# Expert rows loaded, cast and split 1024 columns at a time, a finish of gathered tokens in seven steps, and a power on one column

## Chip, core and metric

The kernel runs on one core of one Trainium2 chip. The metric is the time on the device in microseconds (us). Engines are named as the profile does: PE is TensorE (PEld its weight loads), DVE is VectorE, ACT is ScalarE, POOL is GpSimd, SP is SyncE, which issues most DMAs.

## The reference

One decoder layer over 512 tokens of width 2048: two mixers, then an expert feed-forward (PEER), then a final RMS norm. What matters here is the expert part. Each token picks 8 x 16 of 16384 experts; `u_emb` and `v_emb` are tables of 16384 rows of 2048 floats.

```python
q = (xb @ w_query).reshape(PEER_BLOCK, PEER_HEADS, 2, PEER_HALF)
...
top_s, pos = lax.top_k(cand_s, PEER_TOPK)
eidx = jnp.take_along_axis(cand_i, pos, axis=-1)
gates = jax.nn.softmax(top_s, axis=-1)
u = u_emb[eidx]
act = jax.nn.gelu(jnp.einsum('ld,lhkd->lhk', xb, u), approximate=False)
return jnp.einsum('lhk,lhkd->ld', gates * act, v_emb[eidx])
```

## The kernel before

Up to about 1320 us the mixers run; then the queries and top-k of the expert part (to about 1610 us); the change begins there. The 512 tokens are treated in two ways.

**Dense tokens.** For the first 320 tokens (`TD`) every expert is computed. `expert_u(i)` multiplies 128 rows of u with the tokens: 16 column blocks, each of three 320-column products (`mm3`, lines 203 to 205: high x high, high x low, low x high), so 48 products into one `mm` tile, then a gelu (line 1152). `expert_v(grp)` does 4 such blocks of v: four quarters q of 512 output columns, 48 products each into four `po` tiles, which VectorE adds to `hT` (line 1222). So one expert_u is a **unit** of 48 products, and one quarter of expert_v another. The weights go through `load_split` or its twin in `expert_v`: a DMA of 128 x 512 floats into `wr`/`vr` (10 buffers, `NRAW`), a ScalarE cast to `whi`/`vhi` (line 199), a GpSimd subtraction to `wlo`/`vlo` (line 200), 4 buffers of each (`NSPL`). Such a piece is 12 products.

**Gates.** Before expert_v can begin, `gate_block` builds for every dense token a 128 x 128 table of gates as a product of two one-hot matrices `J` and `I2` (J for four tokens in one VectorE instruction, line 1130; I2 by VectorE for odd tokens, line 1136, and by two ScalarE instructions for even ones, lines 1139 and 1140; product `pg`, line 1141), which goes through DRAM (`glD`) and comes back by group as `gd`. Meanwhile the first 36 expert_u run (`NSP`), their results waiting in DRAM (`actD`). `expert_g` multiplies them with the gates and splits the product into `ghi` and `glo` (8 buffers of each).

**Gathered tokens.** For the last 192 tokens (`TG`) only the chosen rows are fetched: `gather` issues an indirect DMA of 1 MB on GpSimd's queue into one of six `g` buffers (`NGB`). A u token costs VectorE two multiplications of 128 x 1024 (line 1254); a v token costs TensorE four small products `pw` (line 1268). `pace` is called once per unit, 256 times in all (36 in the gate stage, 32 in the first eight groups, which hold only expert_v, then 188), and issues gathers so that the 384 are used up at unit `NGU`. When 64 tokens are done, `end_steps` adds them to the residual and normalises them, in 5 steps of a unit each; its `norm` raises 128 x 64 numbers to -0.5 on GpSimd (line 1309).

Each engine works its queue in order. A scheduler with its own estimate of times sets that order when the program is built, from pool sizes and dependences.

## Time and profile before

| what | us |
|---|---|
| median of 3 runs (lowest, highest) | 4036.59 (4035.16, 4037.14) |
| the profiled execution | 4028.36 |
| its span in the trace | 4026.3 |
| PE busy | 3661.0 (91%) |
| POOL busy | 2547.7 (63%) |
| DVE busy | 2398.0 (60%) |
| ACT busy | 1521.6 (38%) |

Busy time is a mean over stages of different kinds, so it only says that TensorE is the engine to follow. Products overlap in TensorE's pipeline: one lasts longer than the distance to the next, and a stretch that is busy throughout is not yet one in which every product follows at the shortest distance.

### The profile page before, as it was taken

Reading aid. Unit: us, or ns where it says so; the run is one execution under the profiler, and the core shown is the slowest. Engines: PE = TensorE matmul, PEld = TensorE weight load, DVE = VectorE, ACT = ScalarE, POOL = GpSimd, SP = SyncE. Lnnn points to the kernel's source line nnn. Section 1 sums busy time; section 2 is a strip of 40 time slices with the busy share of each in tenths; the row PEclk is TensorE's granted clock in tenths of the full one; section 3 lists DMA queues with packets and bytes.
Section 4 is the critical chain, followed back from the end, with each engine's and each line's share of the span. In section 5 each row is a group of like instructions: output and inputs, shape, how many; then the busy total and the mean of one; then the engine's idle time right before and its main releaser. Section 6 shows DMA issues by size and latency. Waiting matters only on the chain. (4 is left out here: it accounts for less than half of the span.)

```text
span 4026.3 us, 65357 instructions
## 1 busy us (share of the span) xinstructions
PE 3661.0 (91%) x23705; PEld 3044.2 (76%) x23705; DVE 2398.0 (60%) x4504; ACT 1521.6 (38%) x3090; POOL 2547.7 (63%) x1921
## 2 busy tenths in 40 slices
PE   5899999999999896888978999989999998999998
PEld 3667756766657896887867788877888887888898
DVE  7543154666633799988666676665666656642324
ACT  3444323443333411666533333333333333334433
POOL 5445443333315533666767798878888888887676
PEclk8999999998979998999989999989999999999999
DMA  8465653333253322988998999988998998899743
GB/s 335 169 205 189 209 165 75 85 92 116 77 192 93 122 72 66 334 297 296 345 329 313 329 341 347 341 294 322 329 338 318 338 326 312 322 329 305 244 153 121
DMA packets 392370, 964.60 MB, mean 240 GB/s; under 512 B 76080, under 2 KB 141360, under 8 KB 335920
## 3 DMA queue, kind: packets, MB, share of 16 engines
q1 hardware_dynamic: 336752, 557.76, 42.1%
q0 software_dynamic: 55296, 402.68, 26.6%
q8 instruction: 187, 3.06, 0.3%
q14 instruction: 135, 1.11, 0.1%
HBM read 914.34 MB, written 45.94 MB: 239 GB/s over the span
## 5 line engine op out<-in xcount | busy, mean ns | idle before, releaser
L200 POOL TENSOR_TENSOR wlo<-wr,whi 128x512 fp32r<-128x512 f32 (+2 forms) x832 | 1112.9, 1354 | 842.4 <-ACT whi L199 742.0
L200 POOL TENSOR_TENSOR vlo<-vr,vhi 128x512 fp32r<-128x512 f32 x512 | 710.3, 1408 | 204.7 <-ACT vhi L199 177.9
L205 PE MATMUL mm<-n2hi,wlo 128*128 128x320 f32 x2304 | 742.4, 322 | 96.7 <-POOL wlo L200 96.7
L199 ACT CAST whi<-wr 128x512 fp32r<-128x512 f32 (+2 forms) x832 | 501.3, 616 | 682.1 <-PE mm L204 278.0
L203 PE MATMUL mm<-n2hi,whi 128*128 128x320 f32 x2304 | 741.8, 322 | 12.2 <-ACT whi L199 9.7
L1254 DVE SCALAR_TENSOR_TENSOR g<-g,row 128x1024 f32<-128x1024 f32 x384 | 714.8, 1900 | 33.7 <-DMA g<-in_u,eix 33.7
L204 PE MATMUL mm<-n2lo,whi 128*128 128x320 f32 x2304 | 730.4, 317 | 2.4 <-POOL n2lo L200 2.4
L203 PE MATMUL po<-ghi,vhi 128*128 128x320 f32 x2048 | 626.4, 316 | 35.6 <-DVE hT L1222 23.4
L204 PE MATMUL po<-glo,vhi 128*128 128x320 f32 x2048 | 619.6, 311 | 0.0
L205 PEld LDWEIGHTS mm<-n2hi,wlo 128*128 128x128 f32 x2304 | 447.6, 194 | 152.7 <-POOL wlo L200 138.4
L205 PE MATMUL po<-ghi,vlo 128*128 128x320 f32 x2048 | 475.4, 317 | 23.0 <-POOL vlo L200 22.5
L203 PEld LDWEIGHTS mm<-n2hi,whi 128*128 128x128 f32 x2304 | 449.3, 195 | 43.2 <-issue 24.3
L199 ACT CAST vhi<-vr 128x512 fp32r<-128x512 f32 x512 | 308.2, 619 | 431.9 <-PE mm L204 284.1
L204 PEld LDWEIGHTS mm<-n2lo,whi 128*128 128x128 f32 x2304 | 449.3, 195 | 7.6 <-issue 4.2
L203 PEld LDWEIGHTS po<-ghi,vhi 128*128 128x128 f32 x2048 | 388.1, 190 | 84.4 <-DVE hT L1222 35.0
L1222 DVE SCALAR_TENSOR_TENSOR hT<-po,mod,hT 128x320 f32<-128x320 f32 x512 | 248.3, 544 | 304.8 <-PE po L205 226.6
L1179 DVE TENSOR_TENSOR act<-gd,act 128x320 f32<-128x320 f32 x128 | 150.6, 1183 | 449.1 <-ACT act L1152 435.3
L205 PEld LDWEIGHTS po<-ghi,vlo 128*128 128x128 f32 x2048 | 342.0, 190 | 80.3 <-POOL vlo L200 59.5
L204 PEld LDWEIGHTS po<-glo,vhi 128*128 128x128 f32 x2048 | 388.8, 190 | 3.7 <-issue 3.4
L1247 POOL DMA_INDIRECT g<-in_u,eix x192 | 235.1, 1225 | 103.1 <-DMA eix<-exD 30.8
L203 PE MATMUL mm<-nhi,whi 128*128 128x512 f32 x640 | 261.1, 408 | 4.5 <-ACT whi L199 4.5
L205 PE MATMUL mm<-nhi,wlo 128*128 128x512 f32 x640 | 261.3, 408 | 0.0
(437 smaller groups left out, 5762.1 us busy)
## 6 DMA issues: line engine op xcount, KB each, us to landing
wr<-in_uT SPq DMA_DIRECT2D x512, 256.0 KB
vr<-in_v SPq DMA_DIRECT2D x512, 256.0 KB
wr<-in_wrest SPq DMA_DIRECT2D x160, 256.0 KB
aw<-in_ada SPq DMA_DIRECT2D x32, 1024.0 KB
a2w<-in_adar SPq DMA_DIRECT2D x64, 512.0 KB
glD<-gb SPq DMA_DIRECT2D x10, 2048.0 KB
gd<-glD SPq DMA_DIRECT2D x32, 640.0 KB
a3w<-in_adar SPq DMA_DIRECT2D x32, 512.0 KB
```

Source lines behind the costliest of these rows:

```text
L199: copied.append(S.copy(hi, src))
L200: return (eng or V).tensor_tensor(lo, src, hi.bitcast(F32), OP.subtract)
L203: TE.matmul(ps, lhsT=whi, rhs=xhi, start=first, stop=False)
L204: TE.matmul(ps, lhsT=whi, rhs=xlo, start=False, stop=False)
L205: done_mm[0] = TE.matmul(ps, lhsT=wlo, rhs=xhi, start=False, stop=last)
L1179: V.tensor_tensor(a.rearrange("p (b t) -> p b t", t=TB), gd[:, :, i, :], a.rearrange("p (b t) -> p b t", t=TB), OP.mult)
L1222: V.scalar_tensor_tensor(h, po[d], mod2[:, 48 + k:49 + k], h, OP.mult, OP.add)
L1247: G.indirect_dma_start(out=g, out_offset=None, in_=I[s[0]], in_offset=bass.IndirectOffsetOnAxis(ap=ix, axis=0))
L1254: V.scalar_tensor_tensor(g[:, c], g[:, c], 1.0, n2s[i][:, c], OP.mult, OP.mult, accum_out=wtp[:, e, n:n + 1])
```

## The change

- Rows of u, v and the query weights come in pieces of 1024 columns: one DMA of 512 KB, one cast, one subtraction, 24 products. There are 5 raw buffers and 3 split ones of the double size. v comes from a second copy in DRAM, `vq`, in which such a piece is contiguous.
- `expert_v` has 8 steps of 256 output columns with two `po` tiles each instead of 4 with four; `pace` is called after every second one, so units are as before. The pool of `po` keeps 5 tiles.
- `NGU` is 240 instead of 222. `end_steps` has 7 steps; the power works on 64 x 1 numbers and a transposition spreads the result.
- Smaller stores: `act` 5 instead of 6, `ghi` and `glo` 7 instead of 8, `gd` 1 instead of 2; I2 is one tile per token, 4 of them, instead of 2 tiles for four tokens; `ys` has one buffer in the gate stage; one `cand` instead of 2; the index tables keep only dense tokens.

```diff
 TD = 320
-NGU = 222
+NGU = 240
 TG = T - TD
...
 LEAD = 2
-NRAW = 10
-NSPL = 4
-NACT = 6
+NRAW = 5
+NSPL = 3
+NACT = 5
 NSP = 36
...
     out["v"] = l["peer_v"]
+    out["vq"] = l["peer_v"].reshape(32, 4, P, 8, 2, P).transpose(0, 3, 2, 4, 1, 5)
     return {k: np.ascontiguousarray(v) for k, v in out.items()}
...
-        def project_to(pss, ws, xhi, xlo, ahead=()):
+        def project_to(pss, ws, xhi, xlo, ahead=(), step=4):
...
             ahead = list(ahead)
-            for q in range(0, nk, 4):
-                n = min(4, nk - q)
+            for q in range(0, nk, step):
+                n = min(step, nk - q)
                 for j, ps in enumerate(pss):
...
                         mm3(ps, whi[:, i, :], wlo[:, i, :], xhi[k], xlo[k], k == 0, k == nk - 1)
-                if parts:
-                    parts.pop(0)()
+                        if parts and i % 4 == 3:
+                            parts.pop(0)()
             return last
...
         def query(pss, n0):
-            for q in range(0, KT, 4):
+            for q in range(0, KT, 8):
                 for j, ps in enumerate(pss):
-                    whi, wlo, _ = load_split(I["wq"][n0 + j], q, 4)
-                    for i in range(4):
+                    whi, wlo, _ = load_split(I["wq"][n0 + j], q, 8)
+                    for i in range(8):
                         k = q + i
...
                             jT[:, t0:t0 + 4].unsqueeze(2).to_broadcast([P, 4, P]), OP.is_equal)
-            I2 = gx.tile([P, 4, P], F32, name="I2", bufs=2)
             for i in range(4):
+                I2 = gx.tile([P, P], F32, name="I2", bufs=4)
                 t = t0 + i
                 if i % 2:
-                    V.tensor_scalar(I2[:, i], iota, iT[:, t:t + 1], gT[:, t:t + 1], OP.is_equal, OP.mult)
+                    V.tensor_scalar(I2, iota, iT[:, t:t + 1], gT[:, t:t + 1], OP.is_equal, OP.mult)
                 else:
-                    S.activation(I2[:, i], iota, AF.Abs, bias=iT[:, t:t + 1], scale=-1.0)
-                    S.activation(I2[:, i], I2[:, i], AF.Relu, bias=gT[:, t:t + 1], scale=ngT[:, t:t + 1])
-                TE.matmul(ps[:, i], lhsT=J[:, i], rhs=I2[:, i], start=True, stop=True)
+                    S.activation(I2, iota, AF.Abs, bias=iT[:, t:t + 1], scale=-1.0)
+                    S.activation(I2, I2, AF.Relu, bias=gT[:, t:t + 1], scale=ngT[:, t:t + 1])
+                TE.matmul(ps[:, i], lhsT=J[:, i], rhs=I2, start=True, stop=True)
             S.copy(gb[:, :, 4 * q:4 * q + 4], ps.rearrange("p t i -> p i t"))
...
         ps = pu.tile([P, T], F32, name="mm", tag="mm")
-        last = project_to([ps[:, 0:TD]], I["uT"][i:i + 1], nhi, nlo)
+        last = project_to([ps[:, 0:TD]], I["uT"][i:i + 1], nhi, nlo, step=8)
         acts[i] = va.tile([P, TD], F32, name="act")
...
     late = []
-    ended = [0]
     def expert_g(grp):
-        gd = vp.tile([P, TD // TB, 4, TB], F32, name="gd", bufs=2)
+        gd = vp.tile([P, TD // TB, 4, TB], F32, name="gd", bufs=1)
         nc.sync.dma_start(gd, glD.rearrange("b j i t -> j b i t")[:, :, 4 * grp:4 * grp + 4, :])
...
                             a.rearrange("p (b t) -> p b t", t=TB), OP.mult)
-            ghi = vp.tile([P, TD], F32R, name="ghi", bufs=8)
-            glo = vp.tile([P, TD], F32R, name="glo", bufs=8)
+            ghi = vp.tile([P, TD], F32R, name="ghi", bufs=7)
+            glo = vp.tile([P, TD], F32R, name="glo", bufs=7)
             split(ghi, glo, a, V)
...
-    vrows = I["v"].rearrange("(g i j) c -> g j i c", i=4, j=P)
     def expert_v(grp):
...
         gh = ghl.pop(grp)
-        for q in range(4):
-            po = [pv.tile([P, TD], F32, name="po") for _ in range(4)]
+        for q in range(8):
+            vr = wp.tile([P, 2, 4, P], F32, name="vr", tag="wr", bufs=NRAW)
+            nc.sync.dma_start(vr, I["vq"][grp, q])
+            vhi = wp.tile([P, 2, 4, P], F32R, name="vhi", tag="whi")
+            vlo = wp.tile([P, 2, 4, P], F32R, name="vlo", tag="wlo")
+            last = split(vhi, vlo, vr, G)
+            po = [pv.tile([P, TD], F32, name="po") for _ in range(2)]
             for i in range(4):
-                vr = wp.tile([P, 512], F32, name="vr", tag="wr", bufs=NRAW)
-                nc.sync.dma_start(vr, vrows[grp][:, i, 512 * q:512 * q + 512])
-                vhi = wp.tile([P, 512], F32R, name="vhi", tag="whi")
-                vlo = wp.tile([P, 512], F32R, name="vlo", tag="wlo")
-                last = split(vhi, vlo, vr, G)
-                for d in range(4):
-                    cs = slice(P * d, P * d + P)
-                    mm3(po[d], vhi[:, cs], vlo[:, cs], *gh[i], i == 0, i == 3)
-                if parts:
+                for d in range(2):
+                    mm3(po[d], vhi[:, d, i, :], vlo[:, d, i, :], *gh[i], i == 0, i == 3)
+                if parts and i % 2:
                     parts.pop(0)()
-            if grp == 31:
-                sqs = vp.tile([P, 4, TD], F32, name="gd", bufs=2)
-            for d in range(4):
-                k = 4 * q + d
+            if grp == 31 and q % 2 == 0:
+                sqs = vp.tile([P, 4, TD], F32, name="gd", bufs=1)
+            for d in range(2):
+                k = 2 * q + d
                 h = hT[k]
...
                 if grp == 31:
-                    t = sqs[:, d, :] if k else sacc[:, 0:TD]
+                    t = sqs[:, k % 4, :] if k else sacc[:, 0:TD]
                     S.activation(t, h, AF.Square)
...
                         V.tensor_tensor(sacc[:, 0:TD], sacc[:, 0:TD], t, OP.add)
+            if q % 2 == 0:
+                continue
             pace(last)
...
                           start=True, stop=True, tile_position=(0, 32 * q))
-            ys = gq.tile([P, T], F32, name="ys", bufs=2)
+            ys = yp[-1].tile([P, T], F32, name="ys", bufs=len(yp))
             S.copy(ys, ps)
...
         held[0] += 2
+        acc = gq.tile([P, TF], F32, name="acc")
+        rn = gq.tile([TF, 1], F32, name="rnf")
...
+        def total():
+            V.tensor_reduce(acc, sq.rearrange("p k t -> p t k"), mybir.AxisListType.X, OP.add)
         def norm():
-            acc = gq.tile([P, TF], F32, name="acc")
-            V.tensor_reduce(acc, sq.rearrange("p k t -> p t k"), mybir.AxisListType.X, OP.add)
             ps = pu.tile([P, T], F32, name="mm", tag="mm")
-            TE.matmul(ps[:, 0:TF], lhsT=ones, rhs=acc, start=True, stop=True)
-            rn = gq.tile([P, TF], F32, name="rnf")
-            V.tensor_scalar(rn, ps[:, 0:TF], 1.0 / D, 1e-6, OP.mult, OP.add)
-            G.tensor_tensor(rn, rn, negh[:, 0:1].to_broadcast([P, TF]), OP.pow)
+            TE.matmul(ps[0:TF, 0:1], lhsT=acc, rhs=ones[:, 0:1], start=True, stop=True)
+            V.tensor_scalar(rn, ps[0:TF, 0:1], 1.0 / D, 1e-6, OP.mult, OP.add)
+            G.tensor_tensor(rn, rn, negh[0:TF, 0:1], OP.pow)
+        def leave():
+            ps = pu.tile([P, T], F32, name="mm", tag="mm")
+            TE.transpose(ps[:, 0:TF], rn.to_broadcast([TF, P]), ident[0:TF, 0:TF])
             for e in range(2):
                 ks = slice(8 * e, 8 * e + 8)
-                V.tensor_tensor(hg[:, ks], hg[:, ks], rn.unsqueeze(1).to_broadcast([P, 8, TF]), OP.mult)
+                V.tensor_tensor(hg[:, ks], hg[:, ks], ps[:, 0:TF].unsqueeze(1).to_broadcast([P, 8, TF]), OP.mult)
             nc.sync.dma_start(out.rearrange("k p t -> p k t")[:, :, TD + TF * f:TD + TF * f + TF], hg)
             held[0] -= 2
-            ended[0] += 1
-        return [load, lambda: None, lambda: add(0), lambda: add(1), norm]
+        return [load, lambda: None, lambda: add(0), lambda: add(1), total, norm, leave]
...
     vp = st.enter_context(tc.tile_pool(name="vp", bufs=2, side="right", reuse_waits="tile"))
+    yp.append(vp)
     for grp in range(32):
```

What this does to GpSimd's queue is seen around the first power in the middle of the last stage. `wlo` and `vlo` are subtractions, `DMA g` are gathers, `rnf` is the power. Before:

```order
L1247 DMA g<-in_u,eix 128x2048
L1247 DMA g<-in_v,eT 128x2048
L200 TENSOR_TENSOR wlo<-wr,whi 128x512 x2
L200 TENSOR_TENSOR vlo<-vr,vhi 128x512
L1247 DMA g<-in_u,eix 128x2048
L200 TENSOR_TENSOR vlo<-vr,vhi 128x512 x3
L1247 DMA g<-in_v,eT 128x2048
L1309 TENSOR_TENSOR rnf<-rnf,negh 128x64
L200 TENSOR_TENSOR wlo<-wr,whi 128x512 x4
L1247 DMA g<-in_u,eix 128x2048
L1247 DMA g<-in_v,eT 128x2048
L1247 DMA g<-in_u,eix 128x2048
```

After, at the same place:

```order
L1252 DMA g<-in_v,eT 128x2048
L1252 DMA g<-in_u,eix 128x2048
L1252 DMA g<-in_v,eT 128x2048
L202 TENSOR_TENSOR wlo<-wr,whi 128x1024
L1252 DMA g<-in_u,eix 128x2048
L202 TENSOR_TENSOR vlo<-vr,vhi 128x1024 x2
L1252 DMA g<-in_v,eT 128x2048
L1316 TENSOR_TENSOR rnf<-rnf,negh 64x1
L202 TENSOR_TENSOR wlo<-wr,whi 128x1024 x2
L1252 DMA g<-in_u,eix 128x2048
L1252 DMA g<-in_v,eT 128x2048
L202 TENSOR_TENSOR vlo<-vr,vhi 128x1024
```

Two subtractions of 1024 columns stand where four of 512 stood, with as many gathers between them, and the power has shrunk from 128x64 to 64x1.

The second place is the end of the gate stage on ScalarE, where `I` are the one-hot matrices of even tokens, `gb` the gate tables leaving PSUM, `act` the gelu that ends an expert_u, `ys` rows of a gathered token. Before, from the last of the one-hot instructions on:

```order
L1139 ACTIVATE I_16076<-iota,iT 128x128 x2
L1142 COPY gb<-pg 128x128x4
L1140 ACTIVATE I_16076<-I_16076,gT,ngT 128x128 x2
L199 CAST whi<-wr 128x512 x3
L1271 COPY ys<-pw 128x512
L199 CAST whi<-wr 128x512
L1142 COPY gb<-pg 128x128x4
L1152 ACTIVATE act<-mm 128x320
L199 CAST whi<-wr 128x512 x2
L1271 COPY ys<-pw 128x512
L199 CAST whi<-wr 128x512 x2
L1152 ACTIVATE act<-mm 128x320
```

After, from the last gelu of the gate stage on:

```order
L1158 ACTIVATE act<-mm 128x320
L1145 ACTIVATE I_15911<-iota,iT 128x128
L1145 ACTIVATE I_15922<-iota,iT 128x128
L1146 ACTIVATE I_15911<-I_15911,gT,ngT 128x128
L1146 ACTIVATE I_15922<-I_15922,gT,ngT 128x128
L201 CAST vhi<-vr 128x1024
L1145 ACTIVATE I_15929<-iota,iT 128x128
L1146 ACTIVATE I_15929<-I_15929,gT,ngT 128x128
L1145 ACTIVATE I_15940<-iota,iT 128x128
L1146 ACTIVATE I_15940<-I_15940,gT,ngT 128x128
L1145 ACTIVATE I_15947<-iota,iT 128x128
L1146 ACTIVATE I_15947<-I_15947,gT,ngT 128x128
```

Before, six of the 36 gelus (two of them shown) follow the last one-hot matrix. After, none does: the last gelu is followed by 25 of the 160 pairs of one-hot instructions (5 shown). TensorE's queue has moved likewise: before, 168 expert_u products stand behind the last gate product; after, the last 54 gate products have no expert_u product among or behind them.

## Rows read from the trace of the kernel before

**Rows 1.** Engine busy time in six stretches, one per stage: us, busy us and count by engine, clock, DMA.

```profile
1613.00:1978.00 365.00, 318.85 (x2149) 300.42 (x2148) 314.41 (x420) 230.34 (x551) 246.90 (x175) 0.96 0.87 317
1978.00:2029.00 51.00, 34.22 (x214) 27.27 (x212) 15.41 (x24) 14.31 (x28) 33.88 (x26) 0.85 0.98 349
2029.00:2339.00 310.00, 279.80 (x1748) 241.62 (x1748) 211.72 (x301) 101.29 (x189) 237.34 (x179) 0.95 0.91 323
2339.00:3582.00 1243.00, 1143.92 (x7467) 998.19 (x7460) 798.19 (x903) 431.27 (x801) 1043.71 (x779) 0.97 0.91 327
3582.00:3793.00 211.00, 211.00 (x1436) 173.87 (x1436) 46.01 (x72) 87.12 (x156) 154.64 (x129) 1.00 0.89 303
3793.00:4010.00 217.00, 209.25 (x1415) 207.17 (x1413) 74.88 (x114) 88.08 (x160) 157.38 (x114) 0.98 0.43 137
```

**Rows 2.** The same view of single groups of the last stage.

```profile
3862.00:3918.00 56.00, 56.00 (x384) 56.00 (x384) 14.89 (x24) 22.56 (x40) 41.20 (x32) 1.00 0.49 161
2610.00:2770.00 160.00, 138.35 (x890) 122.36 (x890) 103.00 (x115) 51.74 (x96) 126.76 (x94) 0.94 0.86 308
3278.00:3366.00 88.00, 74.64 (x480) 65.75 (x479) 61.43 (x63) 28.41 (x53) 70.62 (x49) 0.92 0.80 271
```

**Rows 3.** The same view, only what writes or reads `pw`: PE, PEld, ACT.

```profile
2029.00:2339.00 310.00, 29.04 (x208) 4.25 (x208) 14.69 (x25) 0.95 0.91 323
2339.00:3582.00 1243.00, 126.19 (x944) 18.40 (x936) 69.15 (x118) 0.97 0.91 327
```

**Rows 4.** Waits of TensorE, 2339 to 3582 us: total us, times, longest.

```profile
PE mm L205 <- POOL wlo L200: 73.4, 51, 7.8
```

**Rows 5.** Waits of TensorE, 2029 to 2339 us.

```profile
PE po L203 <- DVE hT L1222: 23.4, 17, 6.2
```

**Rows 6.** GpSimd's groups by line, 2339 to 3582 us: busy us, mean ns, idle before.

```profile
L200 POOL TENSOR_TENSOR vlo<-vr,vhi 128x512 fp32r<-128x512 f32 x272 | 387.6, 1450 | 83.7 <-ACT vhi L199 66.1 <-PE po L205 10.2 <-DMA vr<-in_v 4.5
L200 POOL TENSOR_TENSOR wlo<-wr,whi 128x512 fp32r<-128x512 f32 x271 | 362.4, 1368 | 33.5 <-ACT whi L199 31.2 <-DMA wr<-in_uT 1.0
L1247 POOL DMA_INDIRECT g<-in_v,eT x120 | 139.9, 1166 | 30.6 <-issue 18.6 <-DMA vr<-in_v 3.0 <-DVE rnf L1308 1.4
```

**Rows 7.** GpSimd's groups by line and shape, whole span.

```profile
L200 POOL TENSOR_TENSOR wlo<-wr,whi 128x512 fp32r<-128x512 f32 x784 | 1053.3, 1360 | 774.0 <-ACT whi L199 673.9 <-DMA mt<-mixD 25.7 <-PE mm L205 12.0
L200 POOL TENSOR_TENSOR wlo<-wr,whi 128x256 fp32r<-128x256 f32 x32 | 25.2, 792 | 33.7 <-ACT whi L199 33.6
L697 POOL TENSOR_TENSOR BK<-BK,WL 128x1024 f32<-128x1024 f32 x8 | 15.2, 1899 | 38.5 <-PE bd L665 38.5
L599 POOL TENSOR_TENSOR rnb<-rnb,negh 128x8 f32<-128x8 f32 x8 | 13.1, 1642 | 12.6 <-DVE rnb L596 10.9 <-PE mm L205 1.7
```

**Rows 8.** VectorE in order of time around 2339 us: start, us.

```profile
2339.23 5.28 DVE L1254 SCALAR_TENSOR_TENSOR g<-g,row 128x1024 f32<-128x1024 f32 x1
...
2344.44 1.21 DVE L1254 SCALAR_TENSOR_TENSOR g<-g,row 128x1024 f32<-128x1024 f32 x1
```

**Rows 9.** GpSimd in order of time at the same place.

```profile
2338.38 5.04 POOL L200 TENSOR_TENSOR vlo<-vr,vhi 128x512 fp32r<-128x512 f32 x4
```

**Rows 10.** GpSimd in order of time, 2655 to 2695 us.

```profile
2661.53 10.59 POOL L1309 TENSOR_TENSOR rnf<-rnf,negh 128x64 f32<-128x64 f32 x1
...
2693.77 1.36 POOL L1247 DMA_INDIRECT g<-in_u,eix  x1 [6.11 <-DMA out<-g]
```

**Rows 11.** VectorE's groups by line, 1613 to 1978 us.

```profile
L1254 DVE SCALAR_TENSOR_TENSOR g<-g,row 128x1024 f32<-128x1024 f32 x92 | 126.8, 1419 | 1.9 <-DMA g<-in_u,eix 1.9
L1136 DVE TENSOR_SCALAR I<-iota,iT,gT 128x128 f32<-128x128 f32 x156 | 122.3, 824 | 0.0
L1130 DVE TENSOR_TENSOR J<-iota,jT 128x512 f32<-128x512 f32 x78 | 78.7, 1009 | 50.2 <-PE pg L1141 50.2
```

**Rows 12.** DMA queues, whole span: packets, MB, share of 16 engines.

```profile
q1 hardware_dynamic: 336752, 557.76, 42.1%
q0 software_dynamic: 55296, 402.68, 26.6%
```

31 lines of the change are left out of this document (18 added, 13 removed).

## The prediction

> **What bounds the kernel now.** I read first the page's busy times, then the view by stretches, because the change leaves the queues as they were until about 1320 us. There the queries and top-k follow, in which VectorE is the bound; the change adds it nothing. So the question starts at 1613 us [rows 1].
>
> To see what TensorE could do at best, take a group without gathers. It is 8 units and lasts 56.0 us with 384 products, TensorE busy throughout [rows 2]: 7.00 us a unit. A v token adds 126.19/118 = 1.07 us (944 products are 118 tokens) [rows 3]. With these two prices each stretch has a floor:
>
> - 2029 to 2339 us, eight groups of expert_v alone: 32 units and 26 tokens, 224 + 28 = 252 us. It lasts 310, so 58 are lost.
> - 2339 to 3582 us, 17 groups: 952 + 126 = 1078 of 1243, 165 lost.
> - 3582 to 3793 us: 24 units and the 36 tokens left, 168 + 38 = 206 of 211, 5 lost.
> - 3793 to 4010 us: 28 units and a token, 197 of 217, 20 lost.
>
> That is 248 us which TensorE loses, and the most that a change after 2029 us can bring.
>
> Next the view of single groups, to split the 165. The groups in which 64 tokens are finished take 160 us for two and 88 for one [rows 2]; the other 14 take (1243 - 248)/14 = 71.1 each, against a floor of 56 + 7.4 = 63.4. So a normal group loses 7.7 us, 0.96 a unit, 131 in 17 groups, and the finishes cost the remaining 34. In those stretches the granted clock is 0.92 to 0.94, that is, TensorE falls to its lower level of 1.2 GHz for a while after it stood still; this is part of the loss.
>
> The chain of waits names the cause for normal groups: TensorE waits for GpSimd's `wlo` [rows 4]. GpSimd needs per unit four subtractions at (387.6 + 362.4)/543 = 1.38 us, and 1.72 gathers (234 in 136 units) at 1.17 [rows 6]: 7.54 us, 95% of TensorE's 63.4/8 = 7.93. Two queues that full, tied by four split buffers, lose time at each delay. From 3582 us on no u row comes and VectorE drops from 798/1243 to 46/211 of the time, GpSimd has 154.64/24 = 6.44 us a unit (75% of 8.6), and TensorE loses 0.2 us a unit, with the DMA engines as busy as before (0.89) [rows 1]. So GpSimd and what disturbs it set the pace, not the DMA.
>
> What disturbs it is VectorE. A multiplication of 128 x 1024 takes 1.21 us, but 5.28 when it begins beside four subtractions, which take 5.04 together [rows 8, 9].
>
> **The change part by part.**
>
> *Until 1613 us:* the queries' bigger pieces start their first product some 2 us later, under VectorE's preparation; single `cand`, and 5 table copies for 3, lie in VectorE's and ScalarE's queues where these are serial anyway. I take 0; without cover it is 3.
>
> *Gate stage, 1613 to 2029 us.* VectorE has 160 I2 at 0.824, 80 J at 1.009 and the u multiplications at 1.419 us [rows 11]. The new order has 98 multiplications ahead of the last I2, the old had 90: 8 x 1.42 = 11 us more on the engine that is the fullest (314 of 365) [rows 1]. I2 has room for 4 tokens instead of 8. VectorE already waits 50.2 us for TensorE to free such tiles [rows 11]; if that doubled it would be 50 more, if the finer tiles free sooner, it falls. Then there is the end: 51 us lie between the last gate product and the first of expert_v (gate table to DRAM and back), and before, TensorE had 34.22 us of work there [rows 1], 168 expert_u products. Now it has some 5 tokens, 5 us. That costs nothing if those products ran earlier in gaps, and up to 29 if they only delayed the gates. I take +15, with -10 and +45 as the bounds.
>
> *Groups of expert_v alone.* Of the 58 lost, 23.4 are waits of TensorE for the addition that empties `po` [rows 5]: with four tiles a step and five in the pool only one is spare. Two tiles a step leave three. I take -25; bounds 0 and -58.
>
> *The split.* The trace has no subtraction of this kind with 1024 columns. From 256 to 512 columns the mean goes from 792 to 1360 ns [rows 7]: 2.22 ns a column and 0.22 us that each instruction costs anyway. A pair of 1.38 thus becomes one of 2.54. A multiplication of 128 x 1024 in another place took 1.90 [rows 7], the lower bound; the upper is no saving, 2.76. GpSimd then needs per unit 2 x 2.54, and 384/240 = 1.60 gathers at 1.17: 6.95 us, against TensorE's 7.00 + 0.80 x 1.07 = 7.86, that is 88% instead of 95%. Drawn as a straight line between the two stretches (75%: 0.2 us lost a unit, 95%: 0.96), 88% loses 0.70; if the loss goes by what is left free (12% against 5%), 0.40. Between them 0.55: 136 x 0.41 = 56 saved, less 6 us because gathers go on 18 units longer. I take -50; bounds 0 and -131. ScalarE's casts are not the bound (431 of 1243) [rows 1], nor is the issue of DMAs.
>
> Here a rule speaks against bigger pieces. The trace: a multiplication that began beside four subtractions waited for all four [rows 8, 9], 5 us of GpSimd's work, and this run is as long with two of 2.54. The Trainium skill, SBUF — State Buffer, section "SBUF: two separate sides", says that VectorE with two SBUF inputs and GpSimd share a port pair which the first takes for the whole instruction. By that alone a wait would end with the instruction, and grow from 1.38 to 2.54 us at most; as an estimate, 128 `glo` subtractions would then lose up to 148 us of VectorE's time, which is idle a third of the stage, and the sum stays.
>
> *Finishes.* The power holds GpSimd for 10.59 us [rows 10]; on 64 x 1 numbers it should cost less than the 1.64 of 128 x 8 [rows 7]. That frees 9 us, three times, when TensorE waits for the same queue: -25 of the 34 + 20 lost; bounds -10 and -45. The wait of 6.11 us of a gather for the leaving store [rows 10] stays, since the two buffers are given back at the same point.
>
> *At nothing:* `ghi` with 7 buffers. The fourth of a group can be cast only when the last step's first products are done; 36 products, 5 us, lie between that and its use, and cast and subtraction need one to two. Without that cover it costs about 1 us a group, 32. `act`, `gd` and `ys` lead by more. The last finish ends 288 products, some 40 us, ahead of the end, so it does not prolong it.
>
> **Sum.** 15 - 25 - 50 - 25 = -85 from the profiled 4028.4: 3943. The median of the runs stands 8.2 higher than that execution, so I predict 3951. All bounds at once give 3795 and 4080.
>
> **The rivals.**
>
> *The DMA engines set the pace.* They are busy 0.91 of the time at 327 GB/s [rows 1]. For it: this leaves little room. Against it: the stretch with 0.89 and no loss. Price: u and v are 268 MB; SP's queue costs 0.421 x 16 x 4026/557.76 = 48.6 engine-us a MB, the gathers 42.6 [rows 12]. At the gathers' price they would save 268 x 6.0/16 = 101 us, half of it as a guess for packets between; with +15 from the gates 4001. The Trainium skill, DMA: Bandwidth & Descriptors, section "Bandwidth", wants transfers of 1 MiB and gives 138 GB/s at 64 KB; transfers of 256 KB, many at a time, reach 327 here, so its table is not this kernel's price.
>
> *Slower: three split buffers are too few.* TensorE may only begin the third product of a piece when all 1024 columns are subtracted, and ScalarE may only cast when a whole piece is free. Each time TensorE catches up, it stands 2.54 - 1.38 = 1.16 us longer. Over 220 units this is 255 us; from a third of the units on it eats the 85. At half of them 4080. For it: the 51 waits on `wlo` of today [rows 4]. Against it: three buffers hold 3072 columns, four held 2048, so GpSimd may be late by more before it counts.
>
> *All loss goes:* if 88% is enough for TensorE to run through, as it does from 3582 us on: 58 + 131 + 34 gone, +15 - 5: about 3820.
>
> *Nothing comes of it:* the gate stage takes what the split gives, about 4035.
>
> **How the numbers follow.** Forecast 0.50, its own range 3885 to 3985. DMA 0.17, all loss gone 0.13, nothing 0.06, slower 0.14. A difference within 0.2% (8 us) counts as none. Faster are the first three, 0.80; same 0.06; slower 0.14. The range from 3850 to 4035 leaves out about half of "all gone" and most of "slower", under 2 in 10.
>
> **What would show it.** Subtractions of 1024 at 2.4 to 2.6 us; normal groups of 67 to 69 us; the first eight groups about 36 each on average instead of 38.75; finishes without the 10.59 us hole; no wait on `hT` ahead of `po`; the first `po` at 2035 to 2055 us. I am wrong if TensorE's waits on `vlo` and `wlo` grow, if `po` begins after 2075 us, or if ScalarE waits for `wr` and `vr` instead.

## The result, and the profile after

The changed kernel takes 4001.1 us (median of 4 runs, 3995.3 to 4007.0) against 4036.9 for the kernel before on the same chip: ratio 0.9906, 95% interval 0.9883 to 0.9929. A second set of runs gave 4001.4 and 0.9888 (0.9868 to 0.9908). It is faster by some 1%, 36 us, where I had forecast 85. One execution of e3_oldpow below and two of the kernel before took 5283 to 11003 us at granted clocks of 0.31 to 0.60; they count in the medians but not in the ratios. The first profiled execution took 4000.3 us with a span of 3998.3.

The view by stretches of the changed kernel, with the stages of [rows 1] (us; busy time of TensorE, its weight loads, VectorE, ScalarE, GpSimd; granted clock; DMA share; GB/s). The rows are the gates, the eight groups of expert_v alone, the 17 mixed groups (expert_u and expert_v) and the end:

```profile
1640.00:2062.00 422.00, 355.76 (x2334) 326.31 (x2332) 344.13 (x437) 249.96 (x509) 250.18 (x127) 0.94 0.82 305
2062.00:2354.00 292.00, 270.87 (x1734) 237.87 (x1735) 234.14 (x294) 93.66 (x125) 211.24 (x112) 0.97 0.89 327
2354.00:3539.00 1185.00, 1123.09 (x7414) 990.62 (x7413) 768.14 (x868) 387.47 (x521) 942.94 (x492) 0.98 0.90 328
3539.00:3998.00 459.00, 434.69 (x2939) 378.64 (x2937) 201.04 (x252) 163.25 (x227) 318.55 (x167) 0.99 0.75 267
```

GpSimd's groups in the mixed stretch (busy us, mean ns, idle before and who ended it), the answer to [rows 6, 7]:

```profile
L202 POOL TENSOR_TENSOR wlo<-wr,whi 128x1024 fp32r<-128x1024 f32 x136 | 341.7, 2530 | 47.1 <-ACT whi L201 45.2 <-PE po L206 0.7
L202 POOL TENSOR_TENSOR vlo<-vr,vhi 128x1024 fp32r<-128x1024 f32 x136 | 337.8, 2494 | 116.7 <-ACT vhi L201 115.3
L1252 POOL DMA_INDIRECT g<-in_u,eix x109 | 136.5, 1252 | 40.7 <-PE mm L207 10.6 <-issue 9.3 <-DVE g L1259 9.0
...
L1316 POOL TENSOR_TENSOR rnf<-rnf,negh 64x1 f32<-64x1 f32 x2 | 1.2, 590 | 0.0
```

TensorE's waits (total, times, longest) in the mixed groups, answering [rows 4], and in the groups of expert_v alone, answering [rows 5]:

```profile
PE mm L207 <- POOL wlo L202: 28.0, 23, 1.6
PE po L207 <- POOL vlo L202: 20.3, 25, 3.2
PE po L206 <- DVE glo L202: 7.5, 3, 2.5
...
PE po L205 <- DVE hT L1224: 18.9, 9, 4.9
```

At first sight my sum held in its parts and only its size was off. The subtraction of 1024 costs 2.50 and 2.53 us (predicted 2.54), the waits on `wlo` fell from 73.4 us to 28.0, normal groups from 71.1 to 67.75 us, and the power takes 0.59 us instead of 10.59. The experiments show that most of this reading was wrong. The fall of that wait, to begin with, is not the work of the pieces: with pieces of 512 and all else as changed (e5_512, 2340 to 3527 us) it is as short:

```profile
PE mm L207 <- POOL wlo L202: 26.9, 37, 1.6
```

### The profile page after: what moved, and what is told of

It is laid out like the page before. It is cut to its first block, busy times and chain, and to the rows that moved or that the text cites. A ratio compares the mean times of both kernels' runs of the same rounds, so it can differ in the third digit from the quotient of the medians.

```text
span 3998.3 us, 62039 instructions
## 1 busy us (share of the span) xinstructions
PE 3671.5 (92%) x23708; PEld 3046.1 (76%) x23708; DVE 2473.4 (62%) x4503; ACT 1455.9 (36%) x2548; POOL 2385.3 (60%) x1377
## 3 DMA queue, kind: packets, MB, share of 16 engines
q1 hardware_dynamic: 258416, 557.72, 41.5%
## 5 line engine op out<-in xcount | busy, mean ns | idle before, releaser
L202 POOL TENSOR_TENSOR wlo<-wr,whi 128x1024 fp32r<-128x1024 f32 (+3 forms) x544 | 1048.9, 1936 | 890.6 <-ACT whi L201 810.3
L202 POOL TENSOR_TENSOR vlo<-vr,vhi 128x1024 fp32r<-128x1024 f32 x256 | 633.2, 2482 | 265.9 <-ACT vhi L201 261.3
L205 PE MATMUL mm<-n2hi,whi 128*128 128x320 f32 x2304 | 732.5, 318 | 10.8 <-ACT whi L201 7.2
L201 ACT CAST whi<-wr 128x1024 fp32r<-128x1024 f32 (+3 forms) x544 | 454.3, 841 | 622.4 <-PE mm L206 309.1
L205 PE MATMUL po<-ghi,vhi 128*128 128x320 f32 x2048 | 641.3, 318 | 33.8 <-DVE hT L1224 20.7
L206 PE MATMUL po<-glo,vhi 128*128 128x320 f32 x2048 | 638.9, 314 | 10.4 <-DVE glo L202 10.0
L207 PE MATMUL po<-ghi,vlo 128*128 128x320 f32 x2048 | 616.3, 318 | 22.7 <-POOL vlo L202 22.3
L1184 DVE TENSOR_TENSOR act<-gd,act 128x320 f32<-128x320 f32 x128 | 179.1, 1409 | 418.9 <-ACT act L1158 396.9
L207 PEld LDWEIGHTS po<-ghi,vlo 128*128 128x128 f32 x2048 | 382.2, 192 | 72.0 <-POOL vlo L202 49.0
L201 ACT CAST vhi<-vr 128x1024 fp32r<-128x1024 f32 x256 | 267.8, 1048 | 277.9 <-PE po L206 130.0
L1252 POOL DMA_INDIRECT g<-in_v,eT x192 | 221.7, 1155 | 77.4 <-issue 29.5
```

What stands on the lines that cost most here:

```text
L201: copied.append(S.copy(hi, src))
L202: return (eng or V).tensor_tensor(lo, src, hi.bitcast(F32), OP.subtract)
L205: TE.matmul(ps, lhsT=whi, rhs=xhi, start=first, stop=False)
L206: TE.matmul(ps, lhsT=whi, rhs=xlo, start=False, stop=False)
L207: done_mm[0] = TE.matmul(ps, lhsT=wlo, rhs=xhi, start=False, stop=last)
L1184: V.tensor_tensor(a.rearrange("p (b t) -> p b t", t=TB), gd[:, :, i, :], a.rearrange("p (b t) -> p b t", t=TB), OP.mult)
```

## The experiments

All runs in one table: median us, the kernel before on the same chip, ratio with its 95% interval, and the stages of the one profiled execution of each. "Mixers" reaches to the first `rr` of the queries, "queries" to the first gate product, "gates" to the first `po`; the eight groups and the 17 groups end with VectorE's last addition of that group to `hT`; then comes the end. The kernel before has medians of 4034 to 4041 us on the different chips, so kernels from different chips are better compared by their ratios than by their times.

| kernel | us | before | ratio | mixers | queries | gates | 8 groups | 17 groups | end |
|---|---|---|---|---|---|---|---|---|---|
| before | | | | 1313 | 303 | 413 | 310 | 1242 | 445 |
| changed, first profile | 4001.1 | 4036.9 | 0.9906 (0.9883–0.9929) | 1332 | 308 | 422 | 292 | 1185 | 459 |
| e0_after, second profile | 4001.4 | 4040.8 | 0.9888 (0.9868–0.9908) | 1326 | 313 | 424 | 293 | 1181 | 463 |
| e1_input | 4038.7 | 4034.8 | 1.0008 (0.9992–1.0024) | 1354 | 301 | 412 | 295 | 1236 | 445 |
| e2_rows | 4009.5 | 4034.8 | 0.9927 (0.9898–0.9956) | 1327 | 311 | 424 | 293 | 1193 | 462 |
| e3_oldpow | 4008.1 | 4034.8 | 0.9916 (0.9889–0.9944) | 1334 | 310 | 423 | 292 | 1182 | 465 |
| e4_ngu222 | 4015.5 | 4034.8 | 0.9951 (0.9933–0.9968) | 1319 | 309 | 421 | 301 | 1209 | 440 |
| e5_512 | 3986.5 | 4040.8 | 0.9854 (0.9832–0.9877) | 1331 | 300 | 413 | 297 | 1187 | 463 |
| e6_newend | 4004.9 | 4034.1 | 0.9923 (0.9909–0.9937) | 1326 | 302 | 417 | 310 | 1212 | 437 |
| e7_nofin | 3982.0 | 4040.8 | 0.9853 (0.9830–0.9876) | 1322 | 314 | 421 | 293 | 1167 | 458 |
| e9_four | 4019.0 | 4040.8 | 0.9926 (0.9898–0.9955) | 1326 | 314 | 424 | 304 | 1187 | 460 |
| e12_ngu240 | 4028.4 | 4034.9 | 0.9982 (0.9967–0.9997) | 1320 | 302 | 405 | 302 | 1228 | 473 |
| e13_512_222 | 3988.1 | 4034.9 | 0.9881 (0.9850–0.9913) | 1327 | 300 | 415 | 296 | 1218 | 440 |
| e14_halfload | 3965.8 | 4034.9 | 0.9852 (0.9809–0.9894) | 1318 | 314 | 427 | 292 | 1148 | 458 |
| e15_halfsplit | 3928.0 | 4034.9 | 0.9732 (0.9702–0.9762) | 1337 | 309 | 424 | 268 | 1136 | 455 |
| e16_512_four | 3999.9 | 4041.4 | 0.9893 (0.9869–0.9918) | 1326 | 301 | 419 | 303 | 1192 | 462 |
| e17_bigload | 3993.9 | 4041.4 | 0.9866 (0.9836–0.9896) | 1336 | 300 | 416 | 290 | 1190 | 463 |
| e18_512_spl6 | 3982.6 | 4041.4 | 0.9847 (0.9830–0.9865) | 1338 | 306 | 421 | 279 | 1181 | 463 |
| e19_512_dve | 3993.4 | 4041.4 | 0.9891 (0.9869–0.9913) | 1323 | 302 | 412 | 289 | 1193 | 467 |
| e20_pieces | 4064.5 | 4034.1 | 1.0069 (1.0055–1.0083) | 1323 | 309 | 423 | 310 | 1244 | 449 |

### Where the first 20 us came from: e1_input, e0_after

In the first two profiles the changed kernel was 20 us behind where its program was still that of before.

```diff
+    out["vq"] = l["peer_v"].reshape(32, 4, P, 8, 2, P).transpose(0, 3, 2, 4, 1, 5)
...
+    nc.sync.dma_start(vtouch, I["vq"][0, 0][:, 0, 0, 0:8])
```

> The kernel before with the second layout of v as one more input, of which one small read is made at the start and nothing else. Theory (the 20 us by which the changed kernel is behind at 1215 us, where its program is still that of before, are a difference between executions): 4037 us, within 8 of the kernel before. Rival (the new input moves other data in DRAM, and the mixers wait longer for it): about 4057, with the gate stage beginning at 1633 us or later instead of 1613.

> The changed kernel once more, for the others of this call to be compared with, and as a second profile. If the 20 us in the mixers are a difference between executions, the beginning of the gate stage scatters as in the other profiles (1616 to 1656 us so far), while the 17 mixed groups take 1185 us again, within 5.

The time of e1_input is that of the kernel before (4038.7 against 4034.8 us, the interval of the ratio includes 1), as the theory had it. But its gate stage begins at 1655 us, where the rival had it. The mixers of before in the view by stretches (columns as above):

```profile
0.00:1313.00 1313.00, 1212.68 (x7458) 849.90 (x7458) 655.79 (x1548) 486.62 (x1045) 547.39 (x415) 0.93 0.48 154
```

The same stretch of e1_input:

```profile
0.00:1354.00 1354.00, 1256.24 (x7458) 871.84 (x7458) 649.05 (x1547) 486.90 (x1045) 546.61 (x415) 0.91 0.47 149
```

The 7458 products are as many, but not in the same order: with the small read the scheduler ordered the queues of the mixers anew, and those of the stages behind them. So the 41 us between these two rows are no difference between executions of one program, and this run doesn't answer its question for the mixers. The other 19 profiles do. In the mixers the queues of TensorE, ScalarE and GpSimd have the order of before in all of them, and the stage takes from 1313 us (the first profile of before, the fastest) to 1338 (e18_512_spl6):

```profile
0.00:1338.00 1338.00, 1234.64 (x7462) 863.14 (x7462) 645.93 (x1549) 487.26 (x1045) 545.13 (x415) 0.92 0.47 151
```

The seven without the new input have a mean of 1323 us, the twelve with it 1329, and e2_rows, which has the change without the input, begins its gates at 1638 us, the changed kernel at 1640. So the 20 us are in the main a difference between executions, and the two profiles that I compared first were not alike. In e0_after the 17 groups took 1181 us, within the 5 expected.

The eight groups teach the opposite. They take 310 us in the kernel before and 310 again in e6_newend, whose queues have the same order up to there, and 292 and 293 in the two profiles of the changed kernel; the 295 of e1_input belong to another order. With an edit that gives no engine work to speak of, and the new order that came with it, the one profile has this stage 15 us shorter, with no measurable effect on the whole. Differences of that size in a stage between two of the kernels below may come from the order alone.

### The pieces of 1024: e5_512, e20_pieces, e17_bigload, e2_rows

```diff
-NRAW = 5                          # e5_512: back to 512, the rest stays
-NSPL = 3
+NRAW = 10
+NSPL = 4
...
-        last = project_to([ps[:, 0:TD]], I["uT"][i:i + 1], nhi, nlo, step=8)
+        last = project_to([ps[:, 0:TD]], I["uT"][i:i + 1], nhi, nlo)
...
+            for d in range(2):
...
+                nc.sync.dma_start(vr, I["vq"][grp, q, :, d])
...
+                last = split(vhi, vlo, vr, G)
```

> The changed kernel with queries, u and v in pieces of 512 columns (ten raw, four split buffers as before); pairs of po, 240 units and the new finish stay. Theory (a subtraction of 1024 costs GpSimd 0.3 us less than two of 512): 4 x 1.38 + 1.6 x 1.17 = 7.4 us a unit instead of 6.95, the 17 mixed groups take 1215 to 1230 us instead of 1185, in all 4030 to 4045. Rival (240 units and the pairs made the gain): 17 groups of 1185 to 1195, 4001 to 4010.

The theory fell: the 17 groups kept their 1187 us, as the rival had it, and the kernel is 15 us faster than with pieces of 1024 (3986.5 against 4001.4, same chip), which neither had. Queries take 300 us instead of 308 and 313, gates 413 instead of 422 and 424; there the 15 us lie.

```diff
-NGU = 240                          # e20_pieces: pieces alone
+NGU = 222
...
+                    nc.sync.dma_start(vr, vrows[grp][:, i:i + 2, 512 * q:512 * q + 512])
...
-        return [load, lambda: None, lambda: add(0), lambda: add(1), total, norm, leave]
+        return [load, lambda: None, lambda: add(0), lambda: add(1), norm]
```

> The pieces of 1024 alone: four po's, the old finish and 222 units as before; single cand, the I2 of one token, five act, seven ghi and one gd stay as in the changed kernel, since they make the room. My prediction gives 50 less in the groups and 15 more in the gates: 4000. Theory now: 20 more in queries and gates, against that the groups with a finish, which make up for the power's hole, and some 9 us in the normal ones: 4015 to 4035. Rival (pieces gain nothing anywhere): 4050 or more.

The pieces, with what makes room for them, make the kernel of before slower by 0.55 to 0.83%; the rival held. GpSimd's groups by line in its 17 groups, 2365 to 3608 us:

```profile
L200 POOL TENSOR_TENSOR wlo<-wr,whi 128x1024 fp32r<-128x1024 f32 x136 | 338.2, 2504 | 60.9 <-ACT whi L199 57.4 <-PE pw L1273 2.3
L200 POOL TENSOR_TENSOR vlo<-vr,vhi 128x1024 fp32r<-128x1024 f32 x136 | 336.0, 2484 | 111.8 <-ACT vhi L199 110.6
```

TensorE's longest waits there (total, times, longest):

```profile
PE mm L205 <- POOL wlo L200: 61.1, 30, 6.4
PE po L205 <- POOL vlo L200: 18.0, 17, 5.6
PE po L203 <- ACT ghi L199: 8.9, 1, 8.9
PE po L204 <- DVE glo L200: 5.6, 4, 2.4
PE po L203 <- ACT vhi L199: 4.4, 3, 2.1
PE mm L203 <- ACT whi L199: 3.0, 9, 0.4
```

Against [rows 6] the subtractions fell from 750.0 to 674.2 us, by 76, more than the 60 that my price gave (272 x 0.22). But GpSimd's idle time before them, ended by ScalarE's casts, rose from 97.3 to 168.0 us, by 71. What GpSimd saves it waits, and the 17 groups last as long (1244). TensorE's waits on `wlo` are fewer, 30 instead of 51 [rows 4], and longer, 2.0 us each instead of 1.4, as in my rival "three split buffers are too few"; their sum did not grow, as the rival had it, but fell by 12 us. The last four rows, waits on casts and on `glo`, are 21.9 us together; in the kernel before such waits are 3.1, and TensorE stands as long in all (103 us, before 99). This run changed the length of a piece and the number of split buffers (three instead of four) together; a kernel with pieces of 1024 and four of them was not run, so which of the two lengthens the waits is not shown.

```diff
-NSPL = 3                           # e17_bigload: loads of 1024, split by 512
+NSPL = 4
...
+                        if i % 4 == 0:
...
+                            last = split(whi, wlo, wr[:, i:i + 4, :], G)
```

> The changed kernel with loads of 1024 columns as they are, but cast, subtraction and split buffers of 512 (four of them). It tells what the pieces cost in queries and gates: if the long subtraction and cast on the way to the first product, query and gate stage fall by 10 us each, to the 300 and 413 of the kernel with pieces of 512, and the time to 3980 to 3990; if five big raw buffers, that is the loads, they stay at 310 and 423 and the time at 3996 to 4005.

Queries fall to 300 and gates to 416, and the time, 3993.9, lies between the two expectations: it is not the load. But the run took two things back, the length of cast and subtraction and the room for split columns (four buffers of 512 instead of three of 1024). In the queries the changed kernel has a wait of TensorE on the copy `qT`, which stands in ScalarE's queue with the casts:

```profile
PE sc L1039 <- ACT qT L1036: 10.3, 4, 2.9
```

In the kernels with four split buffers of 512 it is 0.9 to 1.1 us. In e18_512_spl6 (below), with short pieces but room for 3072 columns as in the changed kernel, it is back, and queries take 306 us, gates 421:

```profile
PE sc L1039 <- ACT qT L1036: 11.0, 5, 4.2
```

So for the queries at least, the columns that are split ahead explain the cost as well as the length of a piece does.

```diff
-            nc.sync.dma_start(vr, I["vq"][grp, q])
+            nc.sync.dma_start(vr, vrows[grp][:, :, 256 * q:256 * q + 256].rearrange("j i (d c) -> j i d c", d=2))
...
```

> The changed kernel, with v read from its own rows in pieces of 1024 columns (runs of 1 KB instead of one of 4 KB a partition); the second layout is no longer there. Theory (the gain comes from the subtraction of 1024 columns and the pairs of po, not from how v lies): 4001 to 4015 us, normal groups of 67 to 69 us. Rival (the layout carries the gain, by cheaper packets): 4030 or more, normal groups of 71 us. If the new input is what delays the mixers, the gate stage begins 20 us earlier here than in the changed kernel.

The second layout is worth little: 1193 us in the 17 groups, a ratio whose interval overlaps that of the changed kernel. The theory's range held.

### The finish: e6_newend, e3_oldpow, e7_nofin

```diff
-        return [load, lambda: None, lambda: add(0), lambda: add(1), norm]
+        return [load, lambda: None, lambda: add(0), lambda: add(1), total, norm, leave]
```

> The kernel before with the new finish alone (seven steps, power on one column). My prediction's term is 25 us. Theory (with 512-column pieces and four po's GpSimd has no slack to make up for the 10.6 us of the power; it has with the pieces of 1024, which is why the old finish cost nothing there): the groups with a finish fall from 160 and 88 us to about 146 and 75, 4006 to 4014 in all. Rival (the finish is worth as little here as in the changed kernel): 4028 to 4040.

> The changed kernel with the finish of before: five steps, power on 128 x 64. My prediction's term was 25 us for the finishes, that is 4026 us here. Theory after seeing the profile (two groups with a finish cost 15 us over normal ones after, 18 before): 4001 to 4011. Rival (seven steps hold two gather buffers two units longer, which cancels a real gain from the power): the same time as the changed kernel, but the kernel with five steps and the small power, run later, is then about 20 us faster than both.

The fence shows the list of steps in e6_newend; e3_oldpow is the reverse on the changed kernel. The new finish alone takes 29 us off the kernel before (4004.9 against 4034.1, near the theory): 30 in the 17 groups, 8 at the end, with some us lost elsewhere in that execution. Two groups with a finish, each time, which took 160 us [rows 2] and 88 + 71 before:

```profile
2626.00:2781.00 155.00, 143.56 (x941) 125.38 (x941) 105.66 (x115) 52.23 (x97) 126.25 (x98) 0.98 0.94 331
3280.00:3426.00 146.00, 137.25 (x899) 120.05 (x897) 107.50 (x115) 53.25 (x98) 121.26 (x93) 0.98 0.95 336
```

In the changed kernel the old finish costs nothing that is clear of noise (ratio 0.9916, its interval overlaps those of the changed kernel): 1182 us in the 17 groups against 1181 and 1185, although the power again holds GpSimd for 10.6 to 10.8 us. In e3_oldpow two groups with a finish take 149 us:

```profile
2690.00:2839.00 149.00, 136.96 (x908) 119.53 (x907) 109.50 (x110) 48.90 (x65) 123.70 (x61) 0.98 0.86 327
```

In e12_ngu240, which has the old finish too but pieces of 512 and four `po`, they take 161, at a lower granted clock:

```profile
2672.00:2833.00 161.00, 145.56 (x933) 128.97 (x933) 111.07 (x111) 54.16 (x99) 134.56 (x97) 0.94 0.89 307
```

The hole is made up at once in the one (85.8 us, then 63.6 for the next group) and not in the other (89.7, then 71.5). e20_pieces (83.6 and 78.9) doesn't make it up either, so neither pieces of 1024 alone nor 240 units alone suffice; what in the company of pieces, pairs (two `po` a step) and 240 units lets it was not separated, and the kernel with five steps and the small power that the expectation names was not run.

```diff
+        def bare():
+            nc.sync.dma_start(out.rearrange("k p t -> p k t")[:, :, TD + TF * f:TD + TF * f + TF], hg)
...
-        return [load, lambda: None, lambda: add(0), lambda: add(1), total, norm, leave]
+        return [load, none, none, none, none, none, bare]
```

> The changed kernel without the arithmetic of the finish: it leaves out the adding, squares, sums, power and scaling of the 192 gathered tokens and stores what it loaded; the loads, the store, the seven steps and the two held buffers stay. Theory (the finish costs by the work itself, 19 products of TensorE and 13 VectorE operations in the busiest stretch): the two groups of a finish fall from 152 to 140 us or less, 3 x 12 in all: 3965 to 3980. Rival (the two held buffers and the late gathers cost): still 148 or more, 3990 to 4001.

All of the finish's arithmetic is worth 19 us here (3982.0 against 4001.4), between the two expectations: the first of the two groups falls from 74.4 to 68.5 us, the second, 75.4, stays at 74.7. So some 7 of the 14 us by which the two exceed normal groups (149.8 against 2 x 67.75) are that work; what the rest is was not separated (the two buffers are still held in this kernel).

### Pairs, and 240 units: e9_four, e16_512_four, e4_ngu222, e13_512_222, e12_ngu240

```diff
-            po = [pv.tile([P, TD], F32, name="po") for _ in range(2)]
+            po = [pv.tile([P, TD], F32, name="po") for _ in range(4)]
...
+                    nc.sync.dma_start(vr, vrows[grp][:, i:i + 2, 512 * q:512 * q + 512])   # e9_four, every second i
+                nc.sync.dma_start(vr, vrows[grp][:, i, 512 * q:512 * q + 512])             # e16_512_four, every i
+                for d in range(4):
```

> The changed kernel with four po tiles a step again: a piece of v holds 512 columns of two rows (from v's own rows), one step four pairs of such products. My term for the pairs was 25 us; the two profiles show 16. Theory now (the 310 us of the eight expert_v groups in the first profile were a difference of executions, since the same program took 295 in another): 292 to 300 us there, 4001 to 4012 in all. Rival (the pairs remove a wait): 308 us or more, waits on hT above 20 us, 4017 or more.

> The kernel with pieces of 512 and 240 units (3986.5 us), but with expert_v as before: four po's that run side by side over the four pieces of a step, rows of v. Theory (one po after another, and its addition as soon as it is done, is what the change gains): 17 groups go from 1187 back to 1220 to 1235 us, the eight groups of expert_v alone from 296 to 300 or more, 4020 to 4030 in all. Rival (the finish, the buffers or the place of the store carry it): 1185 to 1195 and 3985 to 3995.

With pieces of 1024 the pairs are worth 18 us (4019.0 against 4001.4, the rival's time), with pieces of 512 some 13 to 16 (3999.9 against 3986.5 by the times, 0.9893 against 0.9854 by the ratios). TensorE's wait on `hT` from 2062 to 3540 us, first in e9_four, then in e0_after:

```profile
PE po L203 <- DVE hT L1226: 25.9, 14, 3.8
PE po L205 <- DVE hT L1224: 18.5, 9, 4.6
```

In the eight groups the pairs bring 6 to 11 us (304 instead of 293, 303 instead of 297), less than the order of the queues may do. The theory of e9_four, that the 310 us were an accident of one execution, fell with its time; its rival's 308 us for the eight groups were not reached either. For the 17 groups of e16_512_four the rival was right, while its time lies between the two: with the new finish they take 1192 us, with the old one (e12_ngu240) 1228.

```diff
-NGU = 240
+NGU = 222
```

> The changed kernel with gathers spread as before (222 units instead of 240). Theory (GpSimd's load sets what a group loses): 1.72 gathers a unit instead of 1.60 raise GpSimd's need from 6.95 to 7.10 us a unit, the normal groups go from 67.75 to about 69.5 us, 14 of them cost 25 us more, and the end, with 37 tokens instead of 48, gives 12 back: about 4012. Rival (the 18 units have no part in it): 4001, groups of 68 us and the tail 12 us shorter.

> The kernel with pieces of 512, pairs of po and the new finish, but 222 units as before. DMA theory: the 17 groups move the bytes of before and take 1225 to 1245 us; the end is 15 us shorter than with 240; 4010 to 4030. Rival (the pairs or the finish carry what the pieces don't): 1190 to 1210 us, 3985 to 4000.

> The kernel before with the one number 240 instead of 222 (gathers spread over 18 more units), all else as before. My prediction's reading (GpSimd sets the pace; with pieces of 512 it needs 4 x 1.38 + 1.6 x 1.17 = 7.4 of TensorE's 7.86 us a unit, 94%): 17 groups of 1225 to 1242 us, 4025 to 4037 in all. New theory (the DMA engines set the pace at about 328 GB/s, and the 17 groups move 4% fewer bytes): 17 groups of 1180 to 1195 us, the end 15 us longer, 3985 to 4000 in all.

On the kernel before 240 gives 6.5 us, with pieces of 512, pairs and the new finish nothing clear of noise (0.9881 and 0.9854), with pieces of 1024 14 us by the times (4015.5 and 4001.4) and 18 to 25 by the ratios, somewhat more than expected for e4_ngu222 (11). Everywhere it takes time from the 17 groups (14 us, 31 and 24 to 28) and gives it to the end (28, 23 and 19 to 23), where about 10 more v tokens are left. The DMA theory fell in both other runs: 1228 instead of 1180 to 1195 us, which is in the range of my first reading, and 1218 instead of 1225 to 1245, with a time in the rival's range.

### GpSimd or the DMA engines: e14_halfload, e15_halfsplit, e18_512_spl6, e19_512_dve

```diff
+            if q % 2 == 0:
                 vr = wp.tile([P, 2, 4, P], F32, name="vr", tag="wr", bufs=NRAW)
                 nc.sync.dma_start(vr, I["vq"][grp, q])
```

> The changed kernel with every second load of a v piece left out: cast, subtraction and products take the piece loaded before once more, so every engine does the work it did and only the DMA engines move 4.2 MB less a group (the output is another one). DMA theory: 17 groups fall from 1181 us to 1075 to 1105, the eight groups of expert_v alone from 292 to 255 to 270, 3830 to 3900 in all. GpSimd theory: 1170 to 1181 and 285 to 292, 3980 to 4001.

```diff
+            if q % 2 == 0:
...
+                last = split(vhi, vlo, vr, G)
+            else:
+                copied.append(S.copy(vhi, vr))
```

> The changed kernel with every second subtraction of v left out (the products take the piece subtracted before; the output is another one): GpSimd does 170 us less in the 17 groups, 942 to 772 us, the loads stay. GpSimd theory: the 17 groups fall to 1080 to 1120 us, 3870 to 3920 in all. DMA theory: 1165 to 1181, 3980 to 4001.

The eight groups and the 17 groups of e14_halfload:

```profile
2059.00:2351.00 292.00, 273.84 (x1745) 237.74 (x1746) 225.50 (x302) 96.68 (x126) 212.80 (x114) 0.97 0.78 276
2351.00:3499.00 1148.00, 1133.32 (x7381) 977.82 (x7381) 814.55 (x864) 395.69 (x520) 950.10 (x488) 1.00 0.87 306
```

The same of e15_halfsplit:

```profile
2071.00:2339.00 268.00, 259.93 (x1724) 232.82 (x1723) 170.01 (x288) 93.87 (x124) 134.66 (x81) 0.98 0.96 355
2339.00:3474.00 1135.00, 1111.10 (x7382) 980.04 (x7378) 674.63 (x867) 391.62 (x519) 785.90 (x419) 0.99 0.93 341
```

In the eight groups the DMA engines are not the bound (a group lacks 2.1 MB, not the 4.2 of the expectation): 276 GB/s instead of 327, and still 292 us. With fewer subtractions they move 355 GB/s and the groups take 268. VectorE does the same work there in 170.01 us instead of 234.14, beside 134.66 us of GpSimd instead of 211.24, and TensorE's wait on its additions falls from 18.9 us to 1.6:

```profile
PE po L205 <- DVE hT L1227: 1.6, 2, 1.3
```

In the 17 groups both matter: 10% fewer bytes (306 x 1148 against 328 x 1185) take 33 to 37 us off, 157 us less of GpSimd 45 to 49; neither reaches the 1067 us of my floor (952 for the units and 115 for the 108 v tokens left there). So the pace there depends on both queues, and neither theory alone holds. How much of the second gain comes through VectorE, which has 675 us there instead of 768, was not separated.

Both of the next edits are shown against e5_512.

```diff
-NSPL = 4                           # e18_512_spl6
+NSPL = 6
...
-                last = split(vhi, vlo, vr, G)      # e19_512_dve
+                last = split(vhi, vlo, vr, V if q % 2 and d else G)
```

> The kernel with pieces of 512 and six split buffers instead of four. If the two full queues, GpSimd and the DMA engines, only miss each other now and then, two more pieces ahead take the waits on vlo and wlo (62 us in the expert_v stages) away in part: 3960 to 3980. If GpSimd itself is too slow, more buffers change nothing: 3982 to 3990.

> The kernel with pieces of 512, in which VectorE does one in four of the subtractions of v. GpSimd has 0.7 us less a unit. By the run that left out half of them (45 us less in the 17 groups, 24 in the eight), a quarter on GpSimd is worth 35 us: 3950 to 3965. Against it VectorE's additions come later by its own subtraction and by what it waits beside GpSimd's: then 3985 to 4000.

Two more split buffers take 18 us off the eight groups and 6 off the 17, but 14 are given back in queries and gates, where the wait on `qT` is back; 3982.6, in the range of "change nothing", is the fastest kernel that does the whole work, not to be told apart from e5_512. VectorE's subtractions are no help: TensorE then waits for VectorE, as its waits from 2040 to 3540 us in e19_512_dve show:

```profile
PE po L207 <- POOL vlo L202: 34.3, 30, 2.7
PE po L207 <- DVE vlo L202: 29.9, 13, 4.7
```

## Why the prediction was off

**The start: "Until 1613 us: I take 0".** The queries became 5 to 13 us longer (308 to 314 in ten profiles, 301 to 303 in four with the old queries), with the pieces of 1024 and the room for 3072 columns; my "without cover it is 3" was too low. The other 20 us of the first comparison were in the main no effect.

**Gates: +15.** The old gates take 405 to 417 us, mean 412 of four profiles; with I2 of one token and splits of 512 412 to 421, mean 416 of six; with splits of 1024 421 to 427, mean 423 of ten. So it is +11, near the forecast, but more of it with the pieces and their room (7) than with I2 and the smaller stores (4, within the scatter). The order of the gelus was less of a change than told above: in the trace four, not six, follow the last one-hot matrix before, which fits the 168 products.

**Groups of expert_v alone: -25.** The wait on the additions was there, and the eight groups fell from 310 to 292 us, but by the runs that have four `po` or pairs and are alike else the pairs have 6 to 11 us of it. After the change the wait on `hT` is still 18.9 us. It depends less on the number of `po` than on VectorE, which is slower beside a busy GpSimd: with half of v's subtractions left out the wait is 1.6 us (e15_halfsplit).

**The split: -50.** This is the step that failed. The price of the instruction was right (2.50 us for 2.54), and GpSimd's saving of 76 us was even larger than mine. What was wrong is that a lower load of GpSimd must lower the loss, "if the loss goes by what is left free". On the kernel before GpSimd's saved time went into waiting for casts, 71 of the 76 us, and TensorE stood as long. In the 17 groups the pieces bring nothing beyond the scatter: 1244 us for 1242 on the kernel before, 1185 and 1181 for 1187 in the changed one, 1209 for 1218 with 222 units. What they cost lies in queries and gates: 28 us in all on the kernel before, room included (0.0069 x 4034), and 15 in the changed one. The term also held the fewer gathers. These did shorten the 17 groups, but gave 19 to 28 us to the end where I allowed 6. Pieces and 240 units taken out of the changed kernel together (e13_512_222) leave its time as it was: 0.9881 against 0.9906 and 0.9888. So the term of 50 measures nothing, with the sign open.

GpSimd's work does count: 157 us less of it took 45 to 49 off the 17 groups (e15_halfsplit). At that rate 76 us would have been worth some 23, as an estimate; work saved by longer instructions did not bring them. I had written the longer waits down as the rival "slower", with 0.14, and set it apart from the forecast, when it was a cost inside it. Why GpSimd waits longer for the casts, the length of a piece or three buffers instead of four, stays open. (Two bounds of the sum were also added up wrongly: they give 3793 and 4072, not 3795 and 4080.)

**Finishes: -25.** Alone it is 29, a hit. In the changed kernel the same finish is worth some 4 to 11 us by the ratios, not clear of noise, with the 17 groups alike, because something in the change lets the kernel make up the hole. My sum added terms that take away one and the same loss.

**The rival of the DMA engines** had 4001, which is the time measured, but not by its mechanism: it rested on cheaper packets for bigger pieces, and pieces of 512 are faster. SP's queue in the changed kernel:

```profile
q1 hardware_dynamic: 258416, 557.72, 41.5%
```

That is 0.415 x 16 x 3998/557.72 = 47.6 engine-us a MB, 48.6 before [rows 12], far from the 42.6 that the rival took. That it came out at the right time was luck. That the engines share the pace of the 17 groups is shown by e14_halfload.

So the gain, 36 us in the first set of runs and 39 in the second, is: the new finish and the pairs, which with 240 units give 54 (e5_512 against before, same chip), less 15 for the pieces of 1024 (same chip again, so that this difference must come out). Measured one by one, the finish (29), the pairs (13) and the 240 units (6.5, both not far from noise) give 49 of the 54. The 240 units count for 6.5 us to some 20 of it, by the company they are in.

## What to carry to other kernels

Two queues that wait for each other through a few buffers don't lose time by the share in which they are busy alone: bigger items, fewer of them in the buffers, saved an engine 76 us here and gave 71 of them to its wait for the next piece. Terms that take away the same wait don't add; put each on the old kernel alone and take each out of the new one. And compare a stage between two profiles only after a stage with the same queues has been compared: here one differed by up to 25 us. See to it that the queues are the same, too; one small read more had them ordered anew, and a stage came out 15 us shorter.
